# A two-layer decoder trunk: every weight set of seven block products in gate/up, none in the down projection, and two of the four weight sums on VectorE

## The chip, the cores and the metric

The program runs on one core of a Trainium2 chip. A core has TensorE (matmuls, PE in the profile), VectorE (DVE), ScalarE (ACT), GpSimd (POOL) and SyncE (SP, which here only issues loads). They run side by side and wait for each other by semaphores; each executes its own instructions in the order in which they stand. The metric is the time of one execution on the device in microseconds (us); of several runs, the median.

## The reference

Two layers, 256 tokens of width 1024, everything in float32. Each layer has two half-step feed-forward parts around a token mixer and a cross-attention into 256 memory rows:

```
def swiglu(h, w_gate, w_up, w_down):
    return (jax.nn.silu(h @ w_gate) * (h @ w_up)) @ w_down
...
for i in range(DEPTH):
    h = h + 0.5 * swiglu(rmsnorm(h, ffn1_norm[i]), ffn1_w_gate[i], ffn1_w_up[i], ffn1_w_down[i])
    ...
    h = h + memory_cross_attention(rmsnorm(h, xa_norm[i]), mem, xa_mem_norm[i], xa_w_q[i], xa_w_kv[i], xa_w_o[i])
    h = h + 0.5 * swiglu(rmsnorm(h, ffn2_norm[i]), ffn2_w_gate[i], ffn2_w_up[i], ffn2_w_down[i])
return rmsnorm(h, final_norm)
```

The hidden width is 2816, so gate and up are 1024 x 2816 each, down is 2816 x 1024. The change concerns the four feed-forward parts (layer 0: first and second; layer 1: first and second).

## The kernel before

**Triple matmuls.** A float32 operand is split into a rounded part hi and a rest lo, both in a format that TensorE takes at its fast rate. `mm3` (L261) makes a product of hi x hi, hi x lo and lo x hi: three matmuls, of 128 rows by 128 columns of the stationary operand against 512 columns for most weights. A weight granule (`Gran`, L205) is 128x1024 elements, that is two 128-row blocks of 512 columns. Its hi is a cast on ScalarE (L224), its lo a subtraction on VectorE (L225). An ordinary granule serves two token halves, 4 triple matmuls (12 matmuls).

**Buffers and order.** Weight blocks of 1 MB (`W`, `Pair`; issue at L161 and L176 on SyncE's queue) lie in six buffers (`wp`), the split parts in four each (`hp`). The granules of the program form one list; `ready` splits a granule `AHEAD` = 2 places before it is used, and a scheduler then sets the instructions of each engine into an order. Small steps behind a product (a copy out of PSUM, a residual, a transpose) are put into the list by `Pipe.after(us, f)`, which runs f when the matmuls written since then add up to that many estimated us.

**Seven products for eight** (`seven`, L361). Two weight blocks side by side, two k halves high (B11, B12 over B21, B22, each 512x512), and the two token halves of x form a 2x2 product of blocks. Seven triple-matmul products of 512 columns do for the usual eight, with sums of weight blocks (x1 = B11 + B12, x2 = x1 + B22, x4 = x2 + B21, x3 = B12 + B22) and sums of activation blocks (`combine`, which leaves four mixes s0 to s3). A set has 14 granules with 2 triple matmuls (6 matmuls) each, 28 in all for 32. x1 is made on VectorE in two halves of 128x1024 (L203); x2, x4 and x3 are made in place by a DMA from GpSimd's queue that adds B22, B21, B22 a second time from memory (L200, two issues of 512 KB for each). The products go onto two PSUM banks: 0, then 2 and 4 onto the same; 1, then 3, 5 and 6 onto the same. Order: 0 (x1), 1 (B11), 2 (B22), 3 (x2), 5 (x3), 4 (B21), 6 (x4). After each, `after(i, banks)` copies or subtracts, by `Pipe.after(0.7, ...)`.

**A feed-forward part** (`ffn_hidden`, L777, with `ffn` L915 or `last` L1549). Gate and up have 5.5 chunks of 512 columns. Before the change: chunk 0 of gate and of up as ordinary matmuls (`wide`), then the half chunk 5 and chunks 1 and 2 ordinary (`stream`), and chunks 3 and 4 each as one set of seven. The ordinary granules, here called hosts, are laid between the products of a set (`share`: how many hosts ahead of each product, `even` = 2, 1, 2, 1, 2, 1, 2) so that the set's higher ratio of splits to matmuls is thinned out. Of the down projection, k blocks 0 to 7 are a third set of seven over both column halves, which needs a mix of its own of the hidden chunks 0 and 1 (`hy`, `hs`, L885 and L890); the rest are ordinary granules (`down`). Its products 2, 4 and 6 are written straight into the banks of the ordinary down product.

The results of gate and up pass SiLU (ScalarE), a product with the row scale (VectorE), and `turn` (L873): transposes on TensorE, a hi cast and a lo subtraction (hid_hi, hid_lo).

**Around it.** The residual addition (L585, L587) ends a half of the projection before; 1.3 estimated us later `Norm.add` writes the transposes of the new h (xt), whose splits xh and xl the gate needs. MemKV's set of seven in the cross-attention uses the same `seven` and `Sum`.

Of the kernel before, what the change touches and what calls it, by code (L numbers as in the profile page):

```python
# [15 lines left out]
P = 128  # L16
# [41 lines left out]
def trunk(ctx, tc, a, out):  # L58
# [121 lines left out]
    class Sum:  # L180
# [5 lines left out]
        def load(self):  # L186
# [9 lines left out]
            for k in (0, 2):  # L196
                ks = slice(k, k + 2)
                if self.into == "dma":
                    r0 = (w.k0 + k) * P
                    nc.gpsimd.dma_start(self.t[:, ks, :], w.src[r0:r0 + 2 * P, w.c0:w.c0 + w.n]  # L200
                                        .rearrange("(k p) c -> p k c", p=P), accum_op=ALU.add)
                else:
                    nc.vector.tensor_tensor(self.t[:, ks, :], self.l.t[:, ks, :], w.t[:, ks, :], op=ALU.add)  # L203
# [157 lines left out]
    def seven(b1, b2, x, mix, after, place={}):  # L361
# [4 lines left out]
        x2 = Sum(x1, b22, "dma")  # L366
# [7 lines left out]
        def s(i):  # L374
            return lambda k: tuple(v[:, k * P:(k + 1) * P] for v in pipe.need(mix, i))
        plan = {0: (x1, s(0)), 1: (b11, a(0, 0)), 2: (b22, s(1)), 3: (x2, s(2)), 5: (x3, s(3)), 4: (b21, a(0, 1)),
                6: (x4, a(1, 1))}
        out = []
        for i, (w, lhs) in plan.items():
            for k0 in (0, 2):  # L380
                def step(g, i=i, lhs=lhs, k0=k0):
                    own = i not in place
                    if not k0:
                        banks[i] = place[i]() if not own else banks[ONTO[i]] if i in ONTO else acc("seven")
                    for k in range(k0, k0 + 2):
                        lh, ll = lhs(k)
                        mm3(banks[i], lh, ll, g.hi[:, k - k0, :], g.lo[:, k - k0, :], k == 0 and i < 2, own and k == 3,
                            onto=own and i in ONTO)
                        pipe.pe(0.68)
# [387 lines left out]
    def ffn_hidden(nm, l, norm, fin, extra=None):  # L777
# [36 lines left out]
        def seven_fin(c):  # L814
            us, t = {}, {}

            def after(i, b):
                v = nc.vector

                def copy():  # L820
                    t[i] = work(f"p{i}")
                    nc.scalar.copy(t[i], b[i])
                    if i == 2:
                        nc.scalar.copy(b[2], t[1])

# [5 lines left out]
                def c22():  # L831
                    us[1] = t[0]
                    v.tensor_tensor(t[0], t[0], b[5], op=ALU.subtract)
                    nc.scalar.activation(t[0], t[0], AF.Silu, scale=norm.col[:, 1:2])

# [5 lines left out]
                pipe.after(0.7, {0: copy, 1: copy, 2: copy, 3: c12, 5: c22, 4: lambda: up(0), 6: lambda: up(1)}[i])  # L841
            return after

        hy, hs = [], [None] * 4

        def down_fin():
            t = {}

            def after(i, b):
                v = nc.vector  # L850

                def to_h(r, c, x):
                    v.scalar_tensor_tensor(h[r][c], x, 0.5, h[r][c], op0=ALU.mult, op1=ALU.add)

                def copy():
                    t[0] = work("d0")
                    nc.scalar.copy(t[0], b[0])

                def c12():
                    t[3] = work("d3")  # L860
                    v.tensor_tensor(t[3], t[0], b[3], op=ALU.subtract)
                    to_h(0, 1, t[3])

                def c22():
                    v.tensor_tensor(t[0], t[0], b[5], op=ALU.subtract)
                    to_h(1, 0, b[5])
                    to_h(1, 1, t[0])
                    extras(6)
                if i in (0, 1, 3, 5):
                    pipe.after(0.7, {0: copy, 1: lambda: to_h(0, 0, b[1]), 3: c12, 5: c22}[i])  # L870
            return after

        def turn(c, us, n):  # L873
            for i in range(0, n // P, 2):
# [8 lines left out]
                if c < 2:  # L883
                    hy.append(slot("hy"))
                    nc.scalar.copy(v2(hy[-1]), tp)  # L885
                for j in range(2):
                    hid[4 * c + i + j] = (hi[:, j, :], lo[:, j, :])
            if c == 1:
                combine(hy, hs, [3.0 + 2.5 * i for i in range(7)] + [30.0])
        wg, wu = a[nm + "_w_gate"][l], a[nm + "_w_up"][l]  # L890
        first = {} if units else dict(single=True, eng=nc.gpsimd)
        wide([(wg, 0, 512)], norm, "gate", gate_fin(0), **first)
        wide([(wu, 0, 512)], norm, "up", up_fin(0))
        c = HID // 512
        n = stream([(wg, c * 512, 256), (wu, c * 512, 256)], norm, "gateup", up_fin(c, 256, 256))
        for c in (1, 2):
            n += stream([(wg, c * 512, 512)], norm, "gate", gate_fin(c)) + stream([(wu, c * 512, 512)], norm, "up", up_fin(c))
        s = [seven((wu, c * 512), (wg, c * 512), norm.x, norm.s, seven_fin(c)) for c in (3, 4)]
        wd = a[nm + "_w_down"][l]
        early, held = [], []  # L900
# [6 lines left out]
        d1 = down(wd, 1, [(12, 4), (20, 2)], hid, early, 12, part)  # L907
        d0 = down(wd, 0, [(20, 2), (12, 4), (8, 4), (16, 4)], hid, held, 20, fin)
        seventh = seven((wd, 0), (wd, 512), hid, hs, down_fin(), {2: lambda: early[0], 4: lambda: held[0], 6: lambda: held[1]})
        even = [2, 1, 2, 1, 2, 1, 2]  # L910
        weave(share(n[:11], s[0], even) + share(n[11:] + d1[:2], s[1], even))
        weave(share(d0[:3] + d1[2:] + d0[3:], seventh, [1] * 7))
        return hid, wd

    def ffn(nm, l, norm, nxt, extra=None):  # L915
        fin = upd(0.5, nxt)
        hid, wd = ffn_hidden(nm, l, norm, fin, extra)
        weave(down(wd, 1, [(8, 4), (16, 4)], hid, [], 8, fin))
# [630 lines left out]
    def last(norm):  # L1549
# [55 lines left out]
        def run(*gr):  # L1605
            ready(gr[-1].at + AHEAD)
            last_ = gr[-1].k0 + gr[-1].nk == 20
            for t, c0, c1 in [(0, 0, 512), (1, 0, 256), (1, 256, 512)]:
# [3 lines left out]
                for g in gr:  # L1612
                    for k in range(g.nk):
                        kt = g.k0 + k
                        mms(b, t, g, k, slice(c0, c1), kt, kt == 8, kt == 19)
# [3 lines left out]
        ws = [W(wd, k, 4, 512, 512) for k in (8, 16)]  # L1619
# [76 lines left out]
```

## Time and profile before

| | |
|---|---|
| runs | 1266.5, 1266.62, 1266.51; median 1266.51 us |
| the profiled execution | 1266.38 us, span of its records 1264.6 us |
| granted TensorE clock | 0.999 |
| HBM read | 273.82 MB, 217 GB/s over the span |
| DMA from SyncE's queue / GpSimd's | 229.75 MB / 44.57 MB |
| issues at L200 (weight sums by DMA) | 84 of 512 KB |

A row of a group reads: line, engine, operation, output <- inputs, shapes, count, then busy us in all and mean ns of one, then the engine's idle time just before them and who ended it. A row of the timeline reads: start in us, us, engine, line, operation, and in brackets the idle time before it and its end's cause; matmul records overlap their followers. A row of the waits reads: who <- for whom: us in all, times, longest. Line numbers are those of the kernel before; after the change the lines from L377 on are 2 to 27 lower.

### The profile page before, as it was taken

To read this page: it belongs to the slowest core of one execution; us is meant where nothing else is said; L and a number is where in the kernel's file an instruction comes from. 1 tells how busy PE (TensorE), PEld (TensorE's weight loads), DVE (VectorE), ACT (ScalarE), POOL (GpSimd) and SP (SyncE) were. 2 spreads that over 40 slices of the span, in tenths; PEclk is the share of its full clock that TensorE was granted. 3 is DMA by queue.
4 is the path that set the end of the run, shared out by engine and by line. 5 is a ranking of instruction groups with operands and counts; after the bars stand their busy time and mean duration, and the time that the engine had idled before them with its cause. 6 is when DMAs were issued, how large, how long until landed. Compare 5 with 4: busy or idle time off the path is not lost.

```text
span 1264.6 us, 18278 instructions
## 1 busy us (share of the span) xinstructions
PE 1254.6 (99%) x6787; PEld 1077.8 (85%) x6787; DVE 1028.4 (81%) x1487; ACT 861.6 (68%) x1382; POOL 179.7 (14%) x151
## 2 busy tenths in 40 slices
PE   9999999999999999999999999999999999999997
PEld 6888888788998888888888889999998898888886
DVE  6989877877786778888688976798898987868887
ACT  6767675586676667657667756777877775776763
POOL 1210202100100102101110200022132100201020
PEclk9999999999999999999999999999999999999999
DMA  9988986333774879996889886665634685698792
GB/s 332 281 243 243 287 295 199 124 143 133 213 226 161 203 232 270 235 330 196 239 228 278 247 273 208 200 194 167 200 134 167 163 237 191 180 249 224 244 285 75
DMA packets 161579, 276.08 MB, mean 218 GB/s; under 512 B 7081, under 2 KB 43602, under 8 KB 161490
## 3 DMA queue, kind: packets, MB, share of 16 engines
q1 hardware_dynamic: 137744, 229.75, 53.4%
q0 software_dynamic: 23008, 44.57, 20.2%
q8 instruction: 53, 0.87, 0.3%
q10 hardware_dynamic: 738, 0.59, 0.1%
q14 instruction: 36, 0.29, 0.1%
HBM read 273.82 MB, written 1.08 MB: 217 GB/s over the span
## 4 chain that ended last, share of the span: by engine, by line
PE 96%; DVE 2%; ACT 1%; DMA 1%; issue 1%; POOLq 0%; POOL 0%; ACTq 0%
PE out L262 7%; PE out L264 7%; PE out L263 7%; PE seven L263 6%; PE seven L264 6%; PE seven L262 6%; PE gate L262 3%; PE gate L263 3%; PE gate L264 3%; PE up L263 3%; PE up L262 3%; PE up L264 3%; PE xs L264 2%; PE xs L262 2%; PE xs L263 2%; PE htp L878 1%
## 5 line engine op out<-in xcount | busy, mean ns | idle before, releaser
L225 DVE TENSOR_TENSOR wlo<-w,whi 128x1024 fp32r<-128x1024 f32 (+2 forms) x514 | 625.0, 1222 | 170.2 <-ACT whi L224 161.5
L224 ACT CAST whi<-w 128x1024 fp32r<-128x1024 f32 (+2 forms) x516 | 534.2, 1040 | 276.1 <-PE out L264 95.1
L262 PE MATMUL out<-whi,hid_hi 128*128 128x512 f32 x240 | 94.0, 392 | 0.0
L264 PE MATMUL out<-whi,hid_lo 128*128 128x512 f32 x240 | 93.5, 389 | 0.0
L263 PE MATMUL out<-wlo,hid_hi 128*128 128x512 f32 x240 | 93.4, 389 | 0.0
L200 POOL DMA_DIRECT2D w<-in_ffn_w_gate_dram x32 | 38.9, 1236 | 305.7 <-DVE xl L461 150.4
L262 PE MATMUL seven<-whi,s_hi 128*128 128x512 f32 x208 | 82.3, 396 | 0.0
L264 PE MATMUL seven<-whi,s_lo 128*128 128x512 f32 x208 | 81.2, 390 | 0.0
L263 PE MATMUL seven<-wlo,s_hi 128*128 128x512 f32 x208 | 81.0, 390 | 0.0
L263 PE MATMUL up<-wlo,xh 128*128 128x512 f32 x192 | 74.8, 390 | 0.1
L264 PE MATMUL up<-whi,xl 128*128 128x512 f32 x192 | 74.7, 389 | 0.0
L262 PE MATMUL up<-whi,xh 128*128 128x512 f32 x192 | 74.7, 389 | 0.0
L262 PE MATMUL gate<-whi,xh 128*128 128x512 f32 x184 | 72.3, 393 | 0.0
L263 PE MATMUL gate<-wlo,xh 128*128 128x512 f32 x184 | 71.8, 390 | 0.0
L264 PE MATMUL gate<-whi,xl 128*128 128x512 f32 x184 | 71.7, 390 | 0.0
L264 PEld LDWEIGHTS out<-whi,hid_lo 128*128 128x128 f32 x240 | 45.1, 188 | 9.4
L262 PEld LDWEIGHTS out<-whi,hid_hi 128*128 128x128 f32 x240 | 45.1, 188 | 9.2
L263 PEld LDWEIGHTS out<-wlo,hid_hi 128*128 128x128 f32 x240 | 45.1, 188 | 9.1
L200 POOL DMA_DIRECT2D w<-in_ffn_w_down_dram x24 | 29.1, 1220 | 147.4 <-DVE w L203 88.7
L264 PEld LDWEIGHTS seven<-whi,s_lo 128*128 128x128 f32 x208 | 39.0, 188 | 8.3
L262 PEld LDWEIGHTS seven<-whi,s_hi 128*128 128x128 f32 x208 | 39.1, 188 | 7.5
L263 PEld LDWEIGHTS seven<-wlo,s_hi 128*128 128x128 f32 x208 | 39.1, 188 | 7.4
(416 smaller groups left out, 3241.9 us busy)
## 6 DMA issues: line engine op xcount, KB each, us to landing
w<-in_ffn_w_up_dram SPq DMA_DIRECT2D x40, 1024.0 KB, 7.3
w<-in_ffn_w_down_dram SPq DMA_DIRECT2D x40, 1024.0 KB, 7.5
w<-in_ffn_w_gate_dram SPq DMA_DIRECT2D x38, 1024.0 KB, 5.2
w<-in_ssd_w_in_dram SPq DMA_DIRECT2D x24, 1024.0 KB, 5.5
w<-in_ffn_w_gate_dram POOLq DMA_DIRECT2D x32, 512.0 KB, 9.0
w<-in_xa_w_kv_dram SPq DMA_DIRECT2D x16, 1024.0 KB, 5.1
w<-in_ffn_w_down_dram POOLq DMA_DIRECT2D x24, 512.0 KB, 9.5
w<-in_da_w_in_dram SPq DMA_DIRECT2D x12, 1024.0 KB, 6.7
```

The costliest lines, as they stand in the source:

```text
L200: nc.gpsimd.dma_start(self.t[:, ks, :], w.src[r0:r0 + 2 * P, w.c0:w.c0 + w.n] .rearrange("(k p) c -> p k c", p=P), accum_op=ALU.add)
L224: nc.scalar.copy(hv, src)
L225: self.eng.tensor_tensor(self.lo[:, :, o:o + n], src, hv.bitcast(F32), op=ALU.subtract)
L262: nc.tensor.matmul(o, lhsT=lh, rhs=rh, start=start, stop=False, skip_group_check=onto)
L263: nc.tensor.matmul(o, lhsT=lh, rhs=rl, start=False, stop=False, skip_group_check=onto)
L264: nc.tensor.matmul(o, lhsT=ll, rhs=rh, start=False, stop=stop, skip_group_check=onto)
L878: nc.tensor.transpose(tp[:, j, t * P:(t + 1) * P], us[t][:, (i + j) * P:(i + j + 1) * P], ident)
```

## The change

In gate/up, chunks 2, 3 and 4 of the first feed-forward part of layer 0, and chunks 1 to 4 of the other three parts, are sets of seven. The down projection is ordinary throughout, with its own mix (`hy`, `hs`, `down_fin`) gone. The other three parts keep one `wide` (gate 0); up 0 becomes a host. In those parts the first set starts after gate 0 and one host. The hosts are up 0, the half chunk, and then granules of down whose hidden chunks are done. The counts of hosts ahead of the seven products, in the order of products below, are 2,1,1,1,1,1,1 twice and 2,1,2,1,2,1,1 (first part), and 1,1,1,0,1,1,1 three times and 1,0,1,0,1,0,1 (others).

In these sets x2 is added on VectorE (it loads B22 and adds it in place), and x1 and x2 are one instruction of 128x2048 each; x4 and x3 stay with the DMA. The order of products is 0, 1, 3, 2, 5, 4, 6. The difference `c12`, which read the bank of product 3, is now taken after the copies that follow product 2. The set of the memory keys and values keeps its order and its DMA sums, but its x1 is also one instruction. The side work that hung on the down set (`extras(6)`: the memory load, the memory keys' splits, the final gain) hangs on chunk 4's product 5. The last down granules, woven after the half 0, are k blocks 12 to 19 instead of 8 to 11 and 16 to 19.

In matmuls of 512 columns the program has 4088 before and 4052 after; splits of 128x1024 502 and 520; sums on VectorE 28 of 128x1024 and 32 of 128x2048; sums by DMA 84 and 72 issues.

```
-                if self.into == "dma":
+            if self.into == "dma":
+                for k in (0, 2):
...
-                else:
-                    nc.vector.tensor_tensor(self.t[:, ks, :], self.l.t[:, ks, :], w.t[:, ks, :], op=ALU.add)
+            else:
+                w.load()
+                nc.vector.tensor_tensor(self.t, self.l.t, w.t, op=ALU.add)
...
-    def seven(b1, b2, x, mix, after, place={}):
+    def seven(b1, b2, x, mix, after, order=(0, 1, 2, 3, 5, 4, 6), second="dma"):
...
-        x2 = Sum(x1, b22, "dma")
+        x2 = Sum(x1, b22, second)
...
                     if i == 2:
                         nc.scalar.copy(b[2], t[1])
+                        c12()
...
+        half = stream([(wg, c * 512, 256), (wu, c * 512, 256)], norm, "gateup", up_fin(c, 256, 256))
+        six, eight, ten = [1, 1, 1, 0, 1, 1, 1], [2, 1, 1, 1, 1, 1, 1], [2, 1, 2, 1, 2, 1, 1]
+        if norm is first_norm:
+            wide([(wu, 0, 512)], norm, "up", up_fin(0))
+            n = half + stream([(wg, 512, 512)], norm, "gate", gate_fin(1)) + stream([(wu, 512, 512)], norm, "up", up_fin(1))
+            counts = {2: eight, 3: eight, 4: ten}
+        else:
+            n = stream([(wu, 0, 512)], norm, "up", up_fin(0)) + half
+            counts = {1: six, 2: six, 3: six, 4: [1, 0, 1, 0, 1, 0, 1]}
...
+        d0 = down(wd, 0, [(0, 4), (20, 2), (4, 4), (8, 4), (12, 4), (16, 4)], hid, [], 0, fin)
+        d1 = down(wd, 1, [(0, 4), (20, 2), (4, 4), (8, 4)], hid, [], 0, part)
+        for i, j in ((0, 2), (2, 3), (3, 5), (5, 7)):
+            n += d0[i:j] + d1[i:j]
+        steps = []
+        for c, k in counts.items():
+            s = seven((wu, c * 512), (wg, c * 512), norm.x, norm.s, seven_fin(c), (0, 1, 3, 2, 5, 4, 6), "dve")
+            steps += share(n[:sum(k)], s, k)
+            n = n[sum(k):]
+        weave(steps + d0[7:])
```

What stands on VectorE in the first feed-forward part around products 0 and 1 of its first set. w_438 is B11, w_442 the sum x1 (then x2), w_515 the half chunk, s_lo a rest of a mix, hid_lo of the hidden chunk 0; before:

```order
L225 TENSOR_TENSOR wlo_469<-w_442,whi_468 128x1024
L488 TENSOR_TENSOR s_lo_462<-sraw_452,s_hi_461 128x512
L483 TENSOR_TENSOR sraw_510<-y_261 128x256
L483 TENSOR_TENSOR sraw_510<-y_262 128x256
L882 TENSOR_TENSOR hid_lo_481<-htp_475,hid_hi_480 128x512
L225 TENSOR_TENSOR wlo_514<-w_515,whi_513 128x1024
L225 TENSOR_TENSOR wlo_532<-w_438,whi_531 128x1024
L882 TENSOR_TENSOR hid_lo_492<-htp_486,hid_hi_491 128x512
L225 TENSOR_TENSOR wlo_546<-w_438,whi_545 128x1024
L225 TENSOR_TENSOR wlo_564<-w_515,whi_563 128x1024
```

And after, where w_510 is the half chunk and w_536 is B22:

```order
L225 TENSOR_TENSOR wlo_468<-w_442,whi_467 128x1024
L855 TENSOR_TENSOR hid_lo_480<-htp_474,hid_hi_479 128x512
L225 TENSOR_TENSOR wlo_509<-w_510,whi_508 128x1024
L855 TENSOR_TENSOR hid_lo_489<-htp_483,hid_hi_488 128x512
L225 TENSOR_TENSOR wlo_527<-w_438,whi_526 128x1024
L486 TENSOR_TENSOR s_lo_493<-sraw_414,s_hi_492 128x512
L203 TENSOR_TENSOR w_442<-w_442,w_536 128x2048
L486 TENSOR_TENSOR s_lo_523<-sraw_505,s_hi_522 128x512
L225 TENSOR_TENSOR wlo_542<-w_438,whi_541 128x1024
L225 TENSOR_TENSOR wlo_560<-w_510,whi_559 128x1024
```

Between the two splits of B11 there now stand the sum x2 and two rests of mixes.

VectorE at the end of the cross-attention of layer 0, where the second feed-forward part begins (h_85 and h_87 are the first column half of the residual, xl the rests of the new x); before:

```order
L225 TENSOR_TENSOR wlo<-w,whi 128x1024 x3
L585 TENSOR_TENSOR h_85<-out,h_85 128x512
L585 TENSOR_TENSOR h_87<-out,h_87 128x512
L225 TENSOR_TENSOR wlo<-w,whi 128x1024
L461 SCALAR_TENSOR_TENSOR xl<-xt,cols_111,xh 128x256 x4
```

And after:

```order
L225 TENSOR_TENSOR wlo<-w,whi 128x1024 x2
L203 TENSOR_TENSOR w<-w 128x2048
L225 TENSOR_TENSOR wlo<-w,whi 128x1024
L583 TENSOR_TENSOR h_85<-out,h_85 128x512
L583 TENSOR_TENSOR h_87<-out,h_87 128x512
L225 TENSOR_TENSOR wlo<-w,whi 128x1024
```

The first set's x1 stands ahead of the first split of the new part's gate (the row behind it) and of the two residual additions. The same rows stand at the second part of layer 1.

More of the change, by code (lines that the diff above doesn't have):

```diff
@@ L375, in s @@
             return lambda k: tuple(v[:, k * P:(k + 1) * P] for v in pipe.need(mix, i))
-        plan = {0: (x1, s(0)), 1: (b11, a(0, 0)), 2: (b22, s(1)), 3: (x2, s(2)), 5: (x3, s(3)), 4: (b21, a(0, 1)),
-                6: (x4, a(1, 1))}
+        plan = [(x1, s(0)), (b11, a(0, 0)), (b22, s(1)), (x2, s(2)), (b21, a(0, 1)), (x3, s(3)), (x4, a(1, 1))]
         out = []
-        for i, (w, lhs) in plan.items():
+        for i in order:
+            w, lhs = plan[i]
             for k0 in (0, 2):
                 def step(g, i=i, lhs=lhs, k0=k0):
-                    own = i not in place
                     if not k0:
-                        banks[i] = place[i]() if not own else banks[ONTO[i]] if i in ONTO else acc("seven")
+                        banks[i] = banks[ONTO[i]] if i in ONTO else acc("seven")
                     for k in range(k0, k0 + 2):
                         lh, ll = lhs(k)
-                        mm3(banks[i], lh, ll, g.hi[:, k - k0, :], g.lo[:, k - k0, :], k == 0 and i < 2, own and k == 3,
-                            onto=own and i in ONTO)
+                        mm3(banks[i], lh, ll, g.hi[:, k - k0, :], g.lo[:, k - k0, :], k == 0 and i < 2, k == 3, onto=i in ONTO)
                         pipe.pe(0.68)
@@ L840, in up @@
                         extras(c)
[L841 to L870, printed above, removed]
+                if i != 3:
+                    pipe.after(0.7, {0: copy, 1: copy, 2: copy, 5: c22, 4: lambda: up(0), 6: lambda: up(1)}[i])
             return after
@@ L906, in part @@
             pipe.after(0.7, go)
[L907 to L912, printed above, removed]
+        d0 = down(wd, 0, [(0, 4), (20, 2), (4, 4), (8, 4), (12, 4), (16, 4)], hid, [], 0, fin)
[7 more added lines that the diff above has]
+            n = n[sum(k):]
+        assert not n
+        weave(steps + d0[7:])
         return hid, wd
@@ L917, in ffn @@
         hid, wd = ffn_hidden(nm, l, norm, fin, extra)
-        weave(down(wd, 1, [(8, 4), (16, 4)], hid, [], 8, fin))
+        weave(down(wd, 1, [(12, 4), (16, 4)], hid, [], 12, fin))
     def diff_attention(norm, nxt, kv):
```

24 lines of the change are left out of this document (6 added, 18 removed).

## The prediction

> **What bounds the kernel now.** I read the page first: the busy shares of the engines.
>
> ```profile
> span 1264.6 us, 18278 instructions
> PE 1254.6 (99%) x6787; PEld 1077.8 (85%) x6787; DVE 1028.4 (81%) x1487; ACT 861.6 (68%) x1382; POOL 179.7 (14%) x151
> ```
>
> Then the list of what TensorE waited for, in the whole span:
>
> ```profile
> PE warm L599 <- DVE warm L99: 1.5, 1, 1.5
> PE gateup L263 <- DVE wlo L225: 0.6, 1, 0.6
> PE xs L264 <- DVE xq_lo L1077: 0.6, 1, 0.6
> PE gate L327 <- ACT whi L224: 0.5, 1, 0.5
> PE acs L1298 <- issue: 0.2, 1, 0.2
> ```
>
> TensorE waits 3.4 us in five places. A busy row of pipelined matmuls overlaps the next one, so I take the timeline of TensorE for the real distance, in a stretch of 20 matmuls of 512 columns (first and last shown):
>
> ```profile
> 299.62 0.39 PE L262 MATMUL out<-whi,o_hi 128*128 128x512 f32 x1
> ...
> 303.93 0.39 PE L263 MATMUL out<-wlo,o_hi 128*128 128x512 f32 x1
> ```
>
> 19 distances take 303.93 - 299.62 = 4.31 us: 0.2268 us each, whatever the record's 0.39 says. So the time is a count of matmuls as long as the splits on VectorE and ScalarE come in time. What these cost, by operation and shape:
>
> ```profile
> L225 DVE TENSOR_TENSOR wlo<-w,whi 128x1024 fp32r<-128x1024 f32 x502 | 617.9, 1236 | 164.7 <-ACT whi L224 156.0
> L203 DVE TENSOR_TENSOR w<-w 128x1024 f32<-128x1024 f32 x28 | 33.9, 1218 | 0.0
> L882 DVE TENSOR_TENSOR hid_lo<-htp,hid_hi 128x512 fp32r<-128x512 f32 x44 | 29.2, 684 | 5.2 <-ACT hid_hi L881 5.2
> L837 DVE SCALAR_TENSOR_TENSOR p<-seven,rcol,p 128x512 f32<-128x512 f32 x16 | 11.9, 745 | 0.0
> L833 DVE TENSOR_TENSOR p<-p,seven 128x512 f32<-128x512 f32 x8 | 5.4, 680 | 0.0
> ```
>
> And the second feed-forward part (404 to 583 us), with a dense stretch of the first:
>
> ```profile
> 404.00:583.00 179.00, 179.00 (x821) 148.81 (x820) 145.79 (x166) 121.75 (x156) 24.22 (x19) 1.00 0.87 247
> 94.80:126.40 31.60, 31.60 (x145) 26.26 (x144) 29.47 (x49) 24.35 (x32) 2.41 (x2) 1.00 0.86 244
> ```
>
> The columns after the length are TensorE, weight loads, VectorE, ScalarE, GpSimd, granted clock, DMA share, GB/s. TensorE is full in both; VectorE is at 81% of the part and at 93% of the dense stretch, and TensorE still loses nothing there. That is the measure for what the change asks of VectorE.
>
> **The change part by part.** The sum stands against the profiled execution's own 1266.38 us (span 1264.6 and 1.8 around it); the median of the runs, 1266.51, is 0.13 above.
>
> *Matmuls.* A feed-forward part now has 252 triple matmuls: gate/up 32 (gate 0 and up 0), 16 (half chunk), 64 (chunks 1 and 2), 2 x 28 (sevens); down 84. The first part after the change has 80 + 3 x 28 + 88 = 252 again; the other three have 48 + 4 x 28 + 88 = 248. Saved: 3 x 4 x 3 = 36 matmuls of 512 columns, x 0.2268 = **8.2 us**, all on the path. The transposes stay as many. Nothing but waits can take this back.
>
> *A sum in one instruction.* 2048 elements a row stand in no row. From below, 1.218 + 2 x (1.218 - 0.684) = 2.29 us by the slope between 512 and 1024 elements; from above two of the present ones, 2.44. I take 2.29, the slope.
>
> *VectorE's work in a weave.* One set of seven with six hosts: 20 splits x 1.236, two sums x 2.29, two differences x 0.680, two products x 0.745, two hid_lo x 0.684 = 33.5 us. Its matmuls: (6 x 12 + 14 x 6) x 0.2268 = 35.4 us, so 95% before transposes; the last set with four hosts: 31.0 against 29.9, 104%, followed by eight granules with 12 matmuls and one split each. Now the same sum for a set with eleven hosts and the short sum gives 25 x 1.236 + 2.4 + 4.2 = 37.5 against 49.0. But rows overlap by some 0.09 us an instruction (below, 1.22 us at 35.53, and the next starts at 36.66), which takes 5 to 8% off: about 90% and 97%. The first is what the stretch at 94.8 us already carries for nothing. I price it at 0; the last sets at 0.2 us each for three parts, **0.6 us** (0 to 1 us for each of the fifteen sets, no gain possible: TensorE loses nothing there now). In the third part the 8 ml splits and the ScalarE work of the memory keys move into that last set too; they are inside this range. The weight sums by DMA fall from 84 to 72 issues of 512 KB on GpSimd's queue; no one on the path waits for them now, so that is 0. The B22 load moves ahead on SyncE's queue, to the end of the first product; the moved memory loads (four on SyncE in the first part) and final_gain (two on GpSimd's queue) are due tens of us later: 0. Reordering the products: the difference c12 now follows B22's copy, with one host (12 matmuls, 2.7 us) ahead of the product that writes on into its bank. A copy is this, and the difference 0.68, together 1.3: 0.
>
> ```profile
> L822 ACT COPY p<-seven 128x512 f32<-128x512 f32 x24 | 14.2, 593 | 2.4 <-PE seven L264 2.2
> ```
>
> *First part, the second sum in a tight place.* The only wait of TensorE on a split lies here:
>
> ```profile
> 34.25 2.19 ACT L224 CAST whi<-w 128x1024 fp32r<-128x1024 f32 x2 [4.95 <-DVE w L203]
> ```
>
> ```profile
> 32.92 2.35 DVE L203 TENSOR_TENSOR w<-w 128x1024 f32<-128x1024 f32 x2
> 35.19 0.41 DVE L483 TENSOR_TENSOR sraw<-sraw,y 128x256 f32<-128x256 f32 x1
> 35.53 1.22 DVE L225 TENSOR_TENSOR wlo<-w,whi 128x1024 fp32r<-128x1024 f32 x1
> 36.66 0.42 DVE L483 TENSOR_TENSOR sraw<-sraw,y 128x256 f32<-128x256 f32 x1
> ...
> 40.01 2.35 DVE L225 TENSOR_TENSOR wlo<-w,whi 128x1024 fp32r<-128x1024 f32 x2
> 42.27 0.68 DVE L882 TENSOR_TENSOR hid_lo<-htp,hid_hi 128x512 fp32r<-128x512 f32 x1
> 42.88 2.35 DVE L225 TENSOR_TENSOR wlo<-w,whi 128x1024 fp32r<-128x1024 f32 x2
> 45.14 0.68 DVE L488 TENSOR_TENSOR s_lo<-sraw,s_hi 128x512 fp32r<-128x512 f32 x1
> ```
>
> ```profile
> 41.27 0.50 PE L263 MATMUL gateup<-wlo,xh 128*128 128x512 f32 x1 [0.61 <-DVE wlo L225]
> ```
>
> ```profile
> 45.03 0.39 PE L263 MATMUL seven<-wlo,xh 128*128 128x512 f32 x1
> ```
>
> VectorE works without a pause from 32.9 us on. Until the host's split (done at 41.15) the new order holds the same work, and the cast that has to wait for the whole sum (1.0 us later) only delays product 0 into the wait that is there. But the second split of B11, done at 44.0 now, comes behind hid_lo, a split, two s_lo and the new sum: 41.1 + 0.6 + 1.14 + 0.6 + 2.2 + 0.6 + 1.14 = 47.4, by the pitches of these rows. TensorE wants it at 45.03. **+2.4 us.** From below: the 0.6 us that is there could go, -0.6; from above the whole sum and the 1.0 us, +3.3.
>
> *The sum ahead of the residual addition.* In both second feed-forward parts the order puts the first sum ahead of the residual's L583, which the transposes wait for:
>
> ```profile
> 393.92 1.23 DVE L225 TENSOR_TENSOR wlo<-w,whi 128x1024 fp32r<-128x1024 f32 x1 [1.24 <-ACT whi L224]
> 396.64 1.23 DVE L225 TENSOR_TENSOR wlo<-w,whi 128x1024 fp32r<-128x1024 f32 x1 [1.50 <-ACT whi L224]
> 397.78 1.28 DVE L585 TENSOR_TENSOR h<-out,h 128x512 f32<-128x512 f32 x2
> ...
> 399.44 1.03 PE L537 MATMUL xt<-ident,h 128*128 128x128 f32 x8
> ```
>
> VectorE is free from 395.05 to 396.64. With 2.2 us of sum it comes to the split at 397.25, to the additions at 398.4, and ends them at 399.65 instead of 399.06. TensorE, which reaches the transposes at 399.44, some 0.4 after the additions, loses 0.6: **+1.2 us** for two parts. If the sum must wait for its load, queued behind it are that split, both additions, and all that follows. How long loads take on this line:
>
> ```profile
> DMA to landing us min/median/max: 4.3/5.5/18.4
> ```
>
> ```profile
> 386.38 1.22 DVE L225 TENSOR_TENSOR wlo<-w,whi 128x1024 fp32r<-128x1024 f32 x1 [0.46 <-ACT whi L224]
> ```
>
> The load's buffer is freed by this split, which ends at 387.6, so it lands at about 393.5, in time by the median; 2.2 us late would cost 2.2 in each of the two. Bounds 0 to 4.4.
>
> Sum: -8.2 + 2.4 + 1.2 + 0.6 = -4.0, so 1262.4 us.
>
> **The rivals.** *The whole gain.* VectorE's order hides the waits that I priced, by the 5 to 8% of overlap and by the four granules of split buffers: 1258.2 us, 1257.6 if the present wait at 41 us goes too. For it: TensorE lost nothing at 93% of VectorE. Against: at 41 us there is no slack to hide 2.2 us in.
>
> *Given back by small waits.* Four of the fifteen sets lose 1 us each and the additions 1.1 in each of the two parts: -8.2 + 2.4 + 2.2 + 4 = +0.4, so 1266.8; with one set more or less, and either end of the 2.4, 1264 to 1269. For it: the last sets ask for 97% of VectorE, more than any stretch shown above carries for nothing. Against: each is followed by eight granules that ask for half of it.
>
> *The matmuls do not bind.* The page's weight-load row is at 85%; if that were TensorE's real load, 15% of it would be idle and 36 matmuls less would change nothing: 1266. Against it stands the constant distance of 0.2268 us in the timeline, with 0.188 us of load in each:
>
> ```profile
> L264 PEld LDWEIGHTS out<-whi,hid_lo 128*128 128x128 f32 x240 | 45.1, 188 | 9.4
> ```
>
> The Trainium skill, "Perfetto Trace Analysis", section "Identifying the Most-Contended Engine", says that matmul busy time is a bad measure and to judge by the LDWEIGHTS share instead. By that rule the time stays; this trace does not agree, as such loads give that share with no gap between matmuls.
>
> *Slower: sums that wait for their loads.* In the later weaves a set's first sum needs B12, a gate block, and its buffer is mostly the one in which the set before keeps its x3. That buffer is free after x3's second split, at about the end of product 2; the sum comes after the difference that waits for product 5, 24 matmuls later: 5.4 + 0.68 + a split 1.24 = 7.4 us. Every split behind the sum waits with it on VectorE.
>
> ```profile
> w<-in_ffn_w_gate_dram SPq DMA_DIRECT2D x10, 1024.0 KB, 5.7
> ```
>
> ```profile
> 395.18 0.37 SPq L161 DMA_DIRECT2D w<-in_ffn_w_up_dram  x1
> ```
>
> The first is the median from issue to landing in the part from 404 us, 5.7; with 0.4 for the issue, the second row, it leaves 1.3 us. From product 5's end TensorE then has 36 matmuls, 8.2 us, until x4's first split is due, and VectorE's work up to it is 0.68 + 1.24 + 1.37 + 2.29 + 1.24 = 6.8: 1.4 us more. So a landing 2.7 us later than the median is free; eleven sets follow another set, and 6.6 us (from my forecast to 0.2% slower) is 0.6 in each: from 3.3 us late it decides. At 4.2 us, a landing of 9.9, it is 1.5 x 11 = 16.5 and the time 1279; in half of the sets 1270.5. For it: the longest landing on the line is 18.4, and the part has a DMA share of 0.87. Against: 12 of 84 accumulating transfers go.
>
> That the matmuls are not fewer can be left out: the program's order has 4088 of 512 columns before and 4052 after.
>
> **How the numbers follow.** My forecast 0.48, the whole gain 0.17, given back 0.20, matmuls not binding 0.04, slower 0.11. The likeliest is 1262.4. Its own range, from the bounds, is 1260 to 1264.5. The range runs to the whole gain below (1258.3) and through the given-back case above (1269); left out are half of the slower case's upper part, some of the lowest, together under 0.2. 0.2% is 2.5 us and about what a measurement of this kernel can tell: faster is below 1263.9, slower above 1268.9. Faster: 0.17 and nine tenths of 0.48 = 0.60. Same: the rest of that, the 0.04 and most of 0.20 = 0.26. Slower: 0.11 and the edge of 0.20 = 0.14.
>
> **What would show it.** Matmuls 36 fewer at 0.227 us apart; a wait of TensorE on wlo near 45 us of 2 to 3 us, in the second half of product 1; VectorE's additions before the second feed-forward parts ending about 0.6 us after TensorE wants them, so a wait of xt; no other wait over 0.5 us in the weaves; VectorE's total about 1060 us (18 splits and 32 long sums more, 28 short ones and the down part's mixing less). I am wrong if the sums show waits for DMA, if TensorE waits in every set, or if the matmul distance changes.

## The result: 0.7% slower, and the profile after

| | before | after |
|---|---|---|
| median of the runs, us | 1266.57 | 1276.21 (1272.98 to 1276.76) |
| ratio, 95% interval | | 1.007 (1.0052 to 1.0087) |
| the profiled execution, us | 1266.38 | 1276.76 |
| matmuls of 512 columns | 4088 | 4052 |

The 36 matmuls are gone, 8.2 us, and by the profiled executions 18.5 us came in their place. The engines' busy row of the kernel after:

```profile
span 1274.9 us, 18150 instructions
PE 1254.1 (98%) x6751; PEld 1070.9 (84%) x6751; DVE 1057.5 (83%) x1451; ACT 877.6 (69%) x1394; POOL 161.4 (13%) x139
```

What TensorE waited for, and the new first entry among VectorE's waits:

```profile
PE seven L263 <- DVE wlo L225: 7.8, 8, 1.9
PE up L263 <- DVE lam L721: 1.9, 1, 1.9
PE xs L264 <- DVE xq_lo L1052: 1.2, 1, 1.2
```

```profile
DVE w L203 <- DMA w<-in_ffn_w_gate_dram: 24.6, 11, 4.5
```

Before, no sum waited for a load. Now eleven of the 32 sums on VectorE stand 24.6 us in front of gate blocks, and TensorE waits for the splits behind them. (The row with lam, a small step of the mixer, is such a wait too, the one that ends at 87.5 us: x2, lam and the split stand one behind the other.) The chip's time by stretches in TensorE's timeline, with four kernels of the experiments beside the two. A part runs from its first gate matmul to the first matmul of the step named or of the next gate, the last one to the kernel's last matmul. Each column is one traced execution. The runs of the kernel after lie up to 3.8 us apart, so differences of a few tenths between the denser kernels say little.

| stretch, us | before | after | x2's sum left out | x3's transfer left out | x1 in halves | all three |
|---|---|---|---|---|---|---|
| first part to the mixer's first scores | 214.40 | 220.65 | 214.47 | 218.45 | 218.13 | 214.63 |
| first cross-attention, products xs to xo | 33.20 | 34.82 | 34.66 | 34.30 | 33.37 | 33.07 |
| second part, layer 0 | 178.19 | 178.56 | 177.48 | 176.20 | 178.11 | 175.55 |
| first part, layer 1, to the scan's dt | 190.53 | 190.78 | 188.78 | 187.92 | 190.07 | 187.92 |
| second part, layer 1 | 177.51 | 178.68 | 176.54 | 180.96 | 179.31 | 178.21 |

Twelve matmuls less should make each of the last three rows 2.7 us shorter. In the kernel after they are 0.25 to 1.2 us longer: some 3 to 4 us lost in each, 6.3 in the first part, which has no matmul less, and 1.6 in the cross-attention.

**The tight first set** came as forecast. VectorE and TensorE in the kernel after (w of the L203 row is x2):

```profile
42.83 0.69 DVE L486 TENSOR_TENSOR s_lo<-sraw,s_hi 128x512 fp32r<-128x512 f32 x1
43.43 2.29 DVE L203 TENSOR_TENSOR w<-w 128x2048 f32<-128x2048 f32 x1
45.63 0.69 DVE L486 TENSOR_TENSOR s_lo<-sraw,s_hi 128x512 fp32r<-128x512 f32 x1
46.23 2.36 DVE L225 TENSOR_TENSOR wlo<-w,whi 128x1024 fp32r<-128x1024 f32 x2
```

```profile
44.98 0.61 PE L262 MATMUL gateup<-whi,xh 128*128 128x512 f32 x2
47.51 0.50 PE L263 MATMUL seven<-wlo,xh 128*128 128x512 f32 x1 [1.91 <-DVE wlo L225]
```

Two matmuls in 2.53 us where 0.45 is normal: 2.08 lost, in the second half of product 1, at the split behind x2.

**A late set**, the third of the last part: SyncE issues the B22 load, GpSimd has just issued x3's transfer, VectorE stands in front of x2, TensorE behind it:

```profile
1171.88 0.37 SPq L161 DMA_DIRECT2D w<-in_ffn_w_gate_dram  x1
1173.68 4.43 SPq L161 DMA_DIRECT2D w<-in_ffn_w_down_dram  x2
```

```profile
1170.19 2.44 POOL L199 DMA_DIRECT2D w<-in_ffn_w_gate_dram  x2 [17.54 <-DVE w L203]
```

```profile
1176.50 1.21 DVE L225 TENSOR_TENSOR wlo<-w,whi 128x1024 fp32r<-128x1024 f32 x1
1182.23 2.29 DVE L203 TENSOR_TENSOR w<-w 128x2048 f32<-128x2048 f32 x1 [4.51 <-DMA w<-in_ffn_w_gate_dram]
1184.44 1.22 DVE L225 TENSOR_TENSOR wlo<-w,whi 128x1024 fp32r<-128x1024 f32 x1
```

```profile
1183.43 0.39 PE L262 MATMUL seven<-whi,xh 128*128 128x512 f32 x1
1185.71 0.50 PE L263 MATMUL seven<-wlo,xh 128*128 128x512 f32 x1 [1.90 <-DVE wlo L225]
```

B22 takes 10.3 us to land. From 1171 to 1183 us the DMA engines move 1.04 MB for x3 and 1.73 MB of plain loads, of which B22 is 1.05; the rest is of the two down loads. Just before, from 1169.9 to 1171.8 us, they stand still: the transfers come in bursts, which an average over the part does not show. Over the whole second part their share is even lower than before, 0.84 (413 to 591 us) against 0.87. Yet the loads land later. The median over the gate loads in the second part was 5.7 us before; now, from 413 to 572 us:

```profile
w<-in_ffn_w_gate_dram SPq DMA_DIRECT2D x8, 1024.0 KB, 7.7
```

**The clock.** One of the longer waits is paid twice. After the one that ended at 87.5 us the windows show a granted clock of 0.53 (third figure from the end), and in TensorE's timeline seven matmuls stand 0.43 us apart, which loses 1.4 us:

```profile
86.00:88.00 2.00, 0.52 (x2) 0.48 (x3) 2.00 (x5) 0.92 (x1) 0.00 (x0) 1.00 0.13 50
88.00:91.00 3.00, 3.00 (x9) 2.27 (x9) 3.00 (x5) 0.00 (x0) 0.00 (x0) 0.53 0.00 0
```

### The profile page after: what moved, and what is told of

Its sections match the earlier page's. It is cut to its first block, busy times and chain, and to the rows that moved or that the text cites. A ratio compares the mean times of both kernels' runs of the same rounds, so it can differ in the third digit from the quotient of the medians.

```text
span 1274.9 us, 18150 instructions
## 1 busy us (share of the span) xinstructions
PE 1254.1 (98%) x6751; PEld 1070.9 (84%) x6751; DVE 1057.5 (83%) x1451; ACT 877.6 (69%) x1394; POOL 161.4 (13%) x139
## 4 chain that ended last, share of the span: by engine, by line
PE 78%; DVE 9%; DMA 8%; issue 3%; ACT 2%; POOL 0%; POOLq 0%; DVEq 0%; ACTq 0%; SPq 0%
PE out L263 7%; PE out L264 7%; PE out L262 7%; DMA w<-in_ffn_w_gate_dram 7%; PE seven L263 6%; PE seven L264 6%; PE seven L262 6%; DVE wlo L225 4%; PE xs L264 2%; PE xs L262 1%; PE xs L263 1%; DVE w L203 1%; PE mk L262 1%; PE mk L264 1%; PE mk L263 1%
## 5 line engine op out<-in xcount | busy, mean ns | idle before, releaser
L262 PE MATMUL out<-whi,hid_hi 128*128 128x512 f32 x336 | 132.5, 394 | 0.0
L263 PE MATMUL out<-wlo,hid_hi 128*128 128x512 f32 x336 | 131.3, 391 | 0.7 <-DVE wlo L225 0.6
L264 PE MATMUL out<-whi,hid_lo 128*128 128x512 f32 x336 | 131.4, 391 | 0.0
L203 DVE TENSOR_TENSOR w<-w 128x2048 f32<-128x2048 f32 x32 | 73.2, 2288 | 25.7 <-DMA w<-in_ffn_w_gate_dram 24.6
L263 PE MATMUL seven<-wlo,xh 128*128 128x512 f32 x180 | 71.0, 394 | 7.5 <-DVE wlo L225 7.4
L262 PE MATMUL seven<-whi,xh 128*128 128x512 f32 x180 | 70.1, 390 | 0.0
L264 PE MATMUL seven<-whi,xl 128*128 128x512 f32 x180 | 70.1, 390 | 0.0
L199 POOL DMA_DIRECT2D w<-in_ffn_w_up_dram x30 | 36.6, 1251 | 233.7 <-DVE wlo L225 221.2
L263 PEld LDWEIGHTS seven<-wlo,xh 128*128 128x128 f32 x180 | 33.8, 188 | 17.7 <-DVE wlo L225 10.9
L262 PEld LDWEIGHTS seven<-whi,xh 128*128 128x128 f32 x180 | 33.9, 188 | 7.2
```

The source lines that it names most:

```text
L199: nc.gpsimd.dma_start(self.t[:, k:k + 2, :], w.src[r0:r0 + 2 * P, w.c0:w.c0 + w.n] .rearrange("(k p) c -> p k c", p=P), accum_op=ALU.add)
L203: nc.vector.tensor_tensor(self.t, self.l.t, w.t, op=ALU.add)
L262: nc.tensor.matmul(o, lhsT=lh, rhs=rh, start=start, stop=False, skip_group_check=onto)
L263: nc.tensor.matmul(o, lhsT=lh, rhs=rl, start=False, stop=False, skip_group_check=onto)
L264: nc.tensor.matmul(o, lhsT=ll, rhs=rh, start=False, stop=stop, skip_group_check=onto)
```

## The experiments

The times are medians; the kernel before ran beside each at 1266.7 to 1266.9. The edits are to the kernel after, unless said otherwise, and are cut down to their main lines.

### Where x2 is made

**x2 by DMA again**, in the old order of products:

```diff
-            s = seven(..., (0, 1, 3, 2, 5, 4, 6), "dve")
+            s = seven(..., (0, 1, 2, 3, 5, 4, 6), "dma")
```

> Edit: in all fifteen sets of gate/up the second sum x2 goes back to the accumulating DMA and the products to the order 0, 1, 2, 3, 5, 4, 6; the counts of sets and hosts, the ordinary down projection and x1 in one instruction stay. Theory A (the loss is VectorE standing in front of x2 until the B22 block lands, and the tight place of the first set; both come from x2 being made on VectorE): about 1259, 1257 to 1262. Theory B (VectorE has too much work in the weaves, whatever it waits for): VectorE loses 15 x 2.3 = 34 us of sums, also about 1259. Theory C (sets with so few hosts ask too much of the loads, wherever x2 is made): 1268 to 1275, with TensorE waiting on wlo in the last two sets of each part.

1300.1 us. My theory A is down as I had put it: taking x2 back to the DMA does not bring the time back. x2 on VectorE, with the new order, saves 24 us of what the denser sets would cost. Theory C has TensorE's waits about where they are, mostly in the third and fourth sets, but its 1268 to 1275 is far too low. The stretches from the second part on are 6 to 8 us longer than before, the first part only 3.9 (its wait at 45 us is gone). TensorE's waits, and the landing of x2's and x3's transfers from 412 to 576 us (7.6 us in the second part before):

```profile
PE seven L263 <- DVE wlo L225: 11.6, 10, 3.0
PE seven L262 <- ACT whi L224: 7.0, 4, 2.4
```

```profile
w<-in_ffn_w_gate_dram POOLq DMA_DIRECT2D x14, 512.0 KB, 11.3
```

Why shows in the DMA queues of the kernel before, from 404 to 560 us (packets, MB, share of the 16 engines):

```profile
q1 hardware_dynamic: 14576, 27.86, 51.5%
q0 software_dynamic: 4896, 9.44, 35.0%
```

Of 156 us that is 80 us for 27.86 MB of plain loads, 2.9 us a MB, and 55 us for 9.44 MB of accumulating ones, 5.8 us a MB: twice as much. A block of 1024 KB is 1.049 of these MB, so 3.0 us as a plain load and 6.1 us as an accumulating one. By these prices a set with eleven hosts asks for an estimated 9.5 x 3.0 + 3 x 6.1 = 47 us of DMA beside the 49 us of matmuls of the forecast, 96%. A set with six hosts and three sums asks for 39 beside 35.4: more than the matmuls give it. With x2 on VectorE it asks for 33, 94%, and the fourth set with its four hosts for 30 beside 29.9.

**x2 on VectorE after product 1**, old order:

```diff
-                        for w in {0: (x2, x3), 3: (x4,)}.get(i, ()):
+                        for w in {0: (x3,), 1: (x2,), 3: (x4,)}.get(i, ()):
```

> Edit: x2 stays on VectorE, but the products are in the order 0, 1, 2, 3, 5, 4, 6 and the sum is written after product 1, so B22 is wanted no earlier than for its own product 2. VectorE's work is that of the changed kernel. Theory A (the wait for B22's early load): that wait is gone, about 1260, 1258 to 1264, and VectorE waits under 8 us for gate blocks at the sums. Theory B (VectorE's amount of work): 1272 to 1277, as the changed kernel.

1296.9 us, by neither theory as I had drawn it. I had overlooked that the sum's own call issues B22's load: moved back, the sum waits for all of its landing.

```profile
DVE w L203 <- DMA w<-in_ffn_w_gate_dram: 43.2, 15, 7.0
```

So it does not tell the amount of VectorE's work from its waiting. It shows how dear an instruction that waits for a load is in VectorE's order, and that its first part, 216.9 us, does without the wait at 45 us.

### Buffers, time of issue, and what the transfers cost

**Seven weight buffers; x3's transfer after product 1; B22 loaded with B11 and B12**:

```diff
-wp = ctx.enter_context(tc.tile_pool(name="wp", bufs=6))
+wp = ctx.enter_context(tc.tile_pool(name="wp", bufs=7))
...
-                        for w in {0: (x2, x3), 3: (x4,)}.get(i, ()):
+                        for w in {0: (x2,), 1: (x3,), 3: (x4,)}.get(i, ()):
...
                 self.r.load()
+                if self.early:
+                    self.early.load()
```

> Edit: seven weight-block buffers in place of six (four of the 32 small slots given up for it); nothing else. Theory A, if B22's load is late because its buffer comes free late: the load is issued one block earlier, the waits at the sums go, the tight first set stays: about 1263, 1260 to 1267. Theory A, if it is late because of the other transfers that run at that time: 1270 to 1276. Theory B: 1272 to 1277.

> Edit: the accumulating DMA that makes x3 is written after product 1 in place of product 0, so B22's load does not run beside its 1 MB; nothing else. If B22's landing of some 9 us is made long by x3's transfer: it falls to 5 or 6 us and the time to about 1266, 1263 to 1270. If x3's transfer has no part in it: 1272 to 1278, with a new wait if x3 itself comes late for product 5.

> Edit to the changed kernel: in the fifteen sets B22's load is issued together with those of B11 and B12, a product earlier, out of the same six buffers. Theory R: the waits of x2's sums go and the time is about 1265, 1262 to 1268. Theory D: the DMA engines are as full as before and a block that comes earlier makes others later: 1272 to 1282, with the waits moved to x1's sums or to casts that wait for blocks of hosts.

1279.8, 1275.1 and 1274.8 us; the last two lie within the runs of the kernel after. Neither of the two earlier issues helps. With seven buffers the sums wait 28.5 us, no less. With B22 early they wait 11.8 us, but ScalarE's casts now wait 27 us for blocks of down and up in place of 17: a block that comes sooner makes another late. Of x3's transfer placed later the three later parts gain 2.5 us together, which the first part loses.

**x3's transfer left out.**

```diff
-        x3 = Sum(b12, b22, "dma")
+        x3 = b12
```

> Edit to the changed kernel: the accumulating DMA that makes x3 is left out in the fifteen sets (product 5 uses B12 as it is, so gate/up come out as other numbers); all else stays, VectorE's sums too. Theory D (the blocks land late because the accumulating transfers fill the DMA engines: in the stretch 404 to 560 us of the kernel before, 9.44 MB of them took 35.0% of the time and 27.86 MB of plain loads 51.5%, so twice as long for a MB): 15 MB less of them, landings of gate blocks fall from 7.9 to 5 or 6 us, VectorE's waits at the sums from 24.6 to under 8 us, the time to about 1263, 1260 to 1266; the 2.1 us wait at 45 us stays. Theory R (the loads are issued too late, however fast they land): 1270 to 1276.

1269.9 us, 6.3 less, between the ranges of the two theories. The DMA share from 413 to 570 us falls from 0.86 to 0.75, the median landing of the gate blocks in the second part from 7.7 to 6.0, and the waits at the sums to:

```profile
DVE w L203 <- DMA w<-in_ffn_w_gate_dram: 9.9, 6, 5.4
```

The parts in the middle of the table come within 0.7 and 0.1 us of the 2.7 they should gain, so theory D is borne out there. The last part does not (below). Its 180.96 us hold a TensorE wait of 3.2 us and behind it 13 matmuls 0.43 us apart, at a granted clock of 0.52 from 1202 to 1209 us, which loses another 2.6. The first part keeps most of its loss, so it has another cause.

**x2's sum left out**, B22 loaded as early.

```diff
-                nc.vector.tensor_tensor(self.t, self.l.t, w.t, op=ALU.add)
+                if self.into is None:
+                    nc.vector.tensor_tensor(self.t, self.l.t, w.t, op=ALU.add)
```

> Edit to the changed kernel: the instruction that makes x2 on VectorE is left out (x2 is x1, so gate/up come out as other numbers), while B22 is loaded as early as before. It takes away VectorE's wait for B22 and the 2.3 us of each x2. If the loss comes through VectorE standing in front of x2 and through the tight first set: about 1261, 1258 to 1265, no wait at 45 us. If TensorE loses because splits wait for loads wherever the sums stand: 1269 to 1275.

1265.0 us, 11.2 less. The first part is back at 214.47, so its 6.3 us hang on x2's sum on VectorE: the tight set, and a second set in which x2 waits 3.3 us for B22, until 83.9 (TensorE's wait and the clock above follow from it). In the later parts 1 to 2 us each stay lost.

**x3 on VectorE in place of x2**, after product 2, x2 by DMA:

```diff
-        x2, x3 = Sum(x1, b22, "dve"), Sum(b12, b22, "dma")
+        x2, x3 = Sum(x1, b22, "dma"), Sum(b12, b22, "dve")
...
-                        for w in {0: (x2, x3), 3: (x4,)}.get(i, ()):
+                        for w in {0: (x2,), 2: (x3,), 3: (x4,)}.get(i, ()):
```

> Edit to the changed kernel: of the fifteen sets' sums it is x3, not x2, that VectorE makes, after product 2, when both its blocks must have landed anyway; x2 goes to the accumulating DMA; products in the order 0, 1, 2, 3, 5, 4, 6. As many sums on each side as in the changed kernel. If what costs is that x2 on VectorE wants B22 early: about 1262, 1259 to 1266, no wait at 45 us, VectorE's waits for gate blocks under 12 us, at x1 alone. If the accumulating transfers cost wherever they stand and however few: 1270 to 1278.

1276.6 us, no gain. The waits only change their place: the sums still stand 19.7 us in front of gate blocks.

### The sums on GpSimd

**x2; x2 and x3; x3** on GpSimd, in halves, old order:

```diff
+            elif self.into == "pool":
+                w.load()
+                for k in (0, 2):
+                    nc.gpsimd.tensor_tensor(self.t[:, k:k + 2, :], self.l.t[:, k:k + 2, :], w.t[:, k:k + 2, :], op=ALU.add)
```

> Edit to the changed kernel: x2 is made on GpSimd in two halves of 128x1024 (neither VectorE nor the DMA engines carry it); order 0, 1, 2, 3, 5, 4, 6. By the 1.3 to 1.75 us of the present 128x512 operations on GpSimd one x2 is an estimated 5 to 6 us. If the loss comes through VectorE standing in front of x2: about 1265 as with that sum left out, 1262 to 1268, and GpSimd takes over the waits for gate blocks. If a sum of 6 us comes too late for product 3: 1270 to 1280 with TensorE waiting in product 3.

> Edit to the changed kernel: x2 and then x3 on GpSimd in halves, order 0, 1, 2, 3, 5, 4, 6, so that of the four sums the DMA makes x4 alone and VectorE x1 alone. If both named costs are real (the accumulating transfers and VectorE in front of x2): about 1260, 1257 to 1264. If GpSimd's two sums of 5 to 6 us each come too late: 1270 to 1285, with TensorE waiting in products 3 or 5.

> Edit to the changed kernel: x2 by the accumulating DMA, x3 on GpSimd in halves, order 0, 1, 2, 3, 5, 4, 6; B22 is loaded as early as in the changed kernel. As many accumulating transfers as there, but VectorE makes x1 alone. If VectorE in front of x2 carries the loss: 1264, 1261 to 1268. If the transfers carry it: 1270 to 1276, as with x3 on VectorE.

1287.8, 1335.8 and 1300.1 us: every range that I gave is missed, and the traces show a cost that is in none of them. A sum is 6.6 us, a little more than I estimated, but VectorE's splits take twice as long beside it. With x2 on GpSimd:

```profile
460.71 6.64 POOL L204 TENSOR_TENSOR w<-w 128x1024 f32<-128x1024 f32 x2 [2.23 <-DVE wlo L229]
```

```profile
458.26 3.49 DVE L229 TENSOR_TENSOR wlo<-w,whi 128x1024 fp32r<-128x1024 f32 x3
462.33 7.24 DVE L229 TENSOR_TENSOR wlo<-w,whi 128x1024 fp32r<-128x1024 f32 x3
```

Three splits take 3.49 us before the sum and 7.24 us beside it. Over all splits of the kernel with both sums on GpSimd the mean is 1413 ns, against 1236 before:

```profile
L229 DVE TENSOR_TENSOR wlo<-w,whi 128x1024 fp32r<-128x1024 f32 x520 | 722.7, 1413 | 112.0 <-ACT whi L228 109.8
```

The Trainium skill, "SBUF — State Buffer", section "Who interferes with whom", says that a tensor_tensor with both inputs in SBUF and a GpSimd operation that reads SBUF lock each other out of shared ports. These rows agree. That this is all that the three versions lose by is not shown.

### How dense the sets are

**The kernel before, with x2 on VectorE** in its eight gate/up sets, in two halves as x1 there, order 0, 1, 3, 2, 5, 4, 6; eleven hosts and the down set stay:

```diff
-        x2 = Sum(x1, b22, "dma")
+        x2 = Sum(x1, b22, "dve")
...
-        for i, (w, lhs) in plan.items():
+        for i in (0, 1, 3, 2, 5, 4, 6):
```

> Edit to the kernel before: its eight sets in gate/up make x2 on VectorE in the order 0, 1, 3, 2, 5, 4, 6; the counts of sets, the eleven hosts and the set in down stay. If x2 on VectorE is only dear where few hosts stand between the loads: no wait of over 0.5 us in these sets, 1265 to 1268. If it is dear wherever it stands: 1272 to 1278, with VectorE waiting for gate blocks.

1269.7 us, ratio 1.0022 (1.0012 to 1.0031), between the two cases. The first part is 2.7 us longer, with waits of 0.7 us that end at 47.7 and 101.2 us; the three later stretches are the same to 0.01 us (178.19, 190.53, 177.52), no sum waits for a load, and gate blocks in the second part land in 5.6 us. So x2 on VectorE costs nothing in the later parts where eleven hosts stand in a set. By the prices above such a set asks for 41 us of DMA beside 49, 83%. What x2 costs in the changed kernel thus hangs on the denser sets; of fewer hosts and more DMA for a us of matmuls this run does not tell which.

**Four more hosts in the later parts**, 6, 6, 8, 6 in place of 6, 6, 6, 4 (k blocks 12 to 15 of down, from the tail), alone and with x3's transfer later:

```diff
-            counts = {1: six, 2: six, 3: six, 4: [1, 0, 1, 0, 1, 0, 1]}
+            counts = {1: six, 2: six, 3: eight, 4: six}
```

> Edit to the changed kernel: in the three later parts four more granules of down (k blocks 12 to 15 of both halves) become hosts, so the four sets have 6, 6, 8 and 6 of them in place of 6, 6, 6 and 4, and the tail is four granules shorter. Same matmuls, loads and sums. If what decides is how much DMA a set asks for beside its matmuls: the waits at the sums in the third and fourth sets fall, each of the three parts gains 1 to 2 us, about 1272. If it is the one late B22 whatever the density: no gain, 1275 to 1277.

> Edit to the changed kernel: the 26 hosts of the run beside it, and in the three later parts x3's accumulating transfer is written after product 1 in place of product 0. If both help on their own: about 1270, 1268 to 1272. If x3's transfer was harmless: as the run beside it.

1278.1 and 1276.8 us, no gain, where I had expected about 1272 and 1270. The sums' waits do fall, from 24.6 to 8.1 us (8.5 in the second run), as the density would have it. But the tail that I shortened was a cover too: it hid the transposes of the last hidden chunk, for which TensorE now waits:

```profile
PE htp L851 <- DVE p L838: 4.5, 3, 1.5
```

Two more losses stand in the first run's trace. Ahead of the first part of layer 1, the x1 that stands before the residual additions waits 4.7 us for its load, until 582.4, and TensorE's transposes wait 1.6 us behind it: what the prediction had feared for the second parts. And two of the waits on the transposes are followed by some 3 us at half clock (granted 0.72 over 576 to 582 and 757 to 763 us).

**x1 in halves again**, in all sets, the memory's too:

```diff
+            elif self.into is None:
+                for k in (0, 2):
+                    nc.vector.tensor_tensor(self.t[:, k:k + 2, :], self.l.t[:, k:k + 2, :], w.t[:, k:k + 2, :], op=ALU.add)
```

> Edit to the changed kernel: x1 is made in two halves of 128x1024 again, in all fifteen sets and in those of the memory keys and values; x2 stays whole. If the whole x1 is what makes the first cross-attention 1.6 us longer (its set starts its accumulating transfers later): that stretch goes back from 34.8 to 33.2 us, and the time to about 1274. If it isn't: 34.8 and 1276.

1271.9 us, 4.3 less: 1.5 in the cross-attention, as expected, and 2.5 in the first part, which was not. There the wait at 45 us stays, and the one that ended at 87.5 us is gone: x2 waits 1.85 us for B22 in place of 3.27.

**What helped, put together**, x1 in halves with it, and the same with the hosts dealt 5, 5, 7, 5 (in short; its counts are the last two lines, five is 1, 1, 1, 0, 1, 0, 1):

```diff
+   first part:   order (0, 1, 2, 3, 5, 4, 6), {0: (x3,), 1: (x2,), 3: (x4,)}
+   later parts:  order (0, 1, 3, 2, 5, 4, 6), {0: (x2,), 1: (x3,), 3: (x4,)}
...
-            counts = {1: six, 2: six, 3: six, 4: [1, 0, 1, 0, 1, 0, 1]}
+            counts = {1: five, 2: five, 3: [1] * 7, 4: [1, 0, 1, 1, 1, 0, 1]}
```

> A version put together from what helped: x1 in halves; in the first part x2 after product 1 in the order 0, 1, 2, 3, 5, 4, 6; in the three later parts x3's transfer after product 1. If these add up over the 1272 with halves alone: the first part 216.9 us in place of 218.1, the later parts 1.8 us less in all, about 1269. That is no gain on the kernel before; for one the waits in the later parts would have to go as well.

> As the run beside it, with the 22 hosts of the later parts dealt 5, 5, 7, 5 in place of 6, 6, 6, 4, so the third and fourth sets, where the sums waited, are thinner and the tail stays. If the density of loads in those two sets is what is left: each later part at its 175.5 us (12 matmuls under the kernel before), the time about 1264, under the kernel before. If the waits only move to the first two sets: 1268 to 1270.

1271.3 and 1275.2 us, against about 1269 and 1264 to 1270 expected. The gains do not add up, and no version that computes the reference beat the kernel before. With the hosts shifted, x2 waits no more in the later parts, and TensorE waits for splits of down granules in the fourth set instead.

**All three out**: x1 in halves, x2's sum and x3's transfer left out.

> Edit to the changed kernel: x1 in halves, x2's sum on VectorE left out (B22 is loaded as early as before) and x3's accumulating transfer left out, so gate/up come out as other numbers; sets, hosts, matmuls, splits and loads stay. It closes the account. If the wait through x2's sum, x3's transfer and the whole x1 are all there is of the loss: 12 matmuls less in each of three parts show in full, 1258 to 1260. If sets of six hosts cost by themselves: 1262 or more.

1262.8 us, ratio 0.9967 (0.9956 to 0.9979). By the time alone that is the case of sets that cost by themselves; the stretches say otherwise, but for the last. The second and third part now gain 2.64 and 2.61 of the 2.7 us, the first part and the cross-attention are back. The last part is the exception, as it was with x3's transfer alone left out: x1 of its fourth set waits 4.9 us for B12 (5.4 there).

```profile
1194.37 1.22 DVE L203 TENSOR_TENSOR w<-w 128x1024 f32<-128x1024 f32 x1 [4.93 <-DMA w<-in_ffn_w_gate_dram]
```

In these two runs GpSimd, free of x3, issues the final gain's transfers at 1175 to 1181 us, ahead of that set, where the other kernels issue them at 1199 or later. That they hold B12 up is argued from this, not shown, and a cost of the thin fourth set itself is not ruled out there. The 3.4 us of that part are most of what lies between 1262.8 and 1258.2.

## Why the prediction was wrong

**Matmuls, -8.2 us: right.** With the waits out of the way the two middle parts get within 0.1 us of their share, 2.7 us each.

**One sum of 2048 elements: right.** 2.29 us forecast, 2.288 measured; VectorE's total 1060 forecast, 1057.5 measured.

**The tight first set, +2.4: right**, in place and nearly in size: 2.08 there and 0.55 on product 0's first split (the 1.0 us later cast), less the 0.84 of the wait of before that is gone, 1.8 in all.

**The sum ahead of the residual addition, +1.2: not lost.** VectorE ended the additions as late as forecast, but TensorE had a matmul of the projection to set between the transposes, so the stretch grew by 0.1 us:

```profile
403.45 2.29 DVE L203 TENSOR_TENSOR w<-w 128x2048 f32<-128x2048 f32 x1
405.66 1.22 DVE L225 TENSOR_TENSOR wlo<-w,whi 128x1024 fp32r<-128x1024 f32 x1
406.80 1.28 DVE L583 TENSOR_TENSOR h<-out,h 128x512 f32<-128x512 f32 x2
```

```profile
407.71 0.38 PE L535 MATMUL xt<-ident,h 128*128 128x128 f32 x2
407.85 0.48 PE L262 MATMUL out<-whi,xo_hi 128*128 128x512 f32 x1
408.17 0.84 PE L535 MATMUL xt<-ident,h 128*128 128x128 f32 x6
```

**VectorE's work in a weave at 0, the last sets at 0.6, the DMA at 0: this step failed.** I weighed the new sets against VectorE alone, found 90% and took what a stretch of 93% carried for nothing. That stretch had no instruction of VectorE that waits for a load. The DMA I counted over the whole program, 84 issues against 72, and called it relief. To a us of matmuls there is next to none: fewer hosts to a set mean fewer matmuls beside its four blocks and its sums, and x2's move only about makes up for that (by the estimate above 96% of the matmuls' time with eleven hosts and three sums, 94% with six and two, 101% with four). The landings rose from 5.7 to 7.7 us, and x2 on VectorE made a late one a stop of the engine that all splits go through. Why they rose while the DMA share did not is shown in part: without x3's transfer they are 6.0, with eleven hosts 5.6, and x3's transfer one product later leaves them at 7.7. The waits cost 3 to 4 us in each later part, and in the first part what goes beyond the tight set.

**B22 ahead on SyncE's queue at 0: failed with it.** The rival that decided was the slower one, to which I gave 0.11: sums that wait for their loads, from a landing 3.3 us later than the median on. It had the mechanism and the order of size. It named the wrong block: x1 and B12 waited too, up to 2.6 us, but mostly without loss, and the long waits were x2's for B22, in the one set before the last. The reason it gave against itself, that 12 of 84 accumulating transfers go, is the count that misled the sum.

**x1 in one instruction, priced by its duration alone: failed.** Halved it gives 4.3 us back. By the durations the first half lets the first split start 1.1 us earlier (half of 2.29); that all of the 4.3 comes of this is argued, not shown.

**What no case had** is the clock: 1.4 us in this run, and an estimated 10 in the kernel with x2 by DMA, from its granted clock of 0.991 over 1292 us against 0.999 before.

Open is why the gains of the single edits do not add up in the combined version, and the last part of the runs without x3's transfer.

## What to carry to other kernels

Price a rearrangement against each resource in the stretch where it lands, not over the program: here 12 fewer accumulating transfers in all were next to no relief for a us of matmuls. An engine that works in order and carries everyone's operands should not be the one that waits for a load; ask of each instruction that is moved to it what it waits for, not only how long it takes. Before a tail is filled with useful work, ask what it was hiding.

## What the runs showed of the hardware that was not expected

- Accumulating DMA transfers took 5.8 us of all 16 engines for a MB (10^6 bytes), plain loads 2.9.
- A GpSimd addition of SBUF tiles holds up VectorE's subtractions beside it: 7.24 us for three in place of 3.49.
- After a wait of about 2 us TensorE sometimes ran at half rate for some 3 us, seven matmuls of 0.43 us. In the run after, three waits of 2.05 to 2.08 us had it once; the one at 45 us had it in the run with x1 in halves and not in the run after. With four more hosts, two of three waits of 1.5 us had it. With x3's transfer left out, a wait of 3.2 us was followed by some 7 us of it. The Trainium skill, "TensorE: Matmul & The Clock Gate", section "HAM oscillation — how this bites in real kernels", gives idle gaps over about 3.4 us as what to avoid; the trace differs, 2.06 us were enough.
